# Group A's rotary sums: traced two units later and tied to the instruction ahead of them on their engine

## The chip, the core and the metric

The kernel runs on one core of a Trainium2 chip. A core has a matrix engine (TensorE, PE in the profile, with its weight loads as PEld), three elementwise engines (VectorE as DVE, ScalarE as ACT, GpSimd as POOL), and a queue engine, SyncE (SP), which in this kernel issues most of the DMA transfers. Each engine works through its own list of instructions in order, and an instruction that needs another engine's result waits at the head of that list on a semaphore. The metric is the device time of one execution in microseconds. The program is one two-layer encoder over 512 tokens of width 1024, batch 1.

## What is computed

The reference, cut to the part that the change touches (group A of the even layer):

```
z = h @ w_in
qa, ka, va, cq, ckv, kr = jnp.split(z, EVEN_SPLITS, axis=-1)
qa = axial_rope(rmsnorm(qa.reshape(b, s, A_HEADS, HEAD_DIM), a_q_norm), row, col)
ka = axial_rope(rmsnorm(ka.reshape(b, s, A_KV_HEADS, HEAD_DIM), a_k_norm), row, col)
oa = block_attention(qa, ka, va, HEAD_DIM ** -0.5)     # 8 query heads, 2 key heads, softmax over 512 keys
ob = block_attention(q_full, k_full, vb, ...)          # group B, 8 heads from low-rank latents cq, ckv, kr
h = h + concat(oa, ob) @ w_out
h = h + sq_relu_mlp(rmsnorm(h, norm_ffn[layer]), ...)
...
rope: x * cos + swap(x) * sin, swap exchanging the halves of each rotary pair
```

The odd layer (neighbourhood attention) and both MLPs follow, then a final norm. The change alters no arithmetic.

## The kernel before

All products are done in three passes of a rounded part and its remainder (`hi`, `lo`), which is why so many instructions come in pairs: a copy on ScalarE that rounds, and a subtraction on VectorE that keeps what was lost.

**Units.** `attend` runs heads in units of 128 queries: unit n = 4 x head + block, so group A's eight heads are units 0 to 31. For each unit the code is written in this order: the score matmuls (line 893, two for group A), the head's `done(i)` callback, the row minimum with scaling on VectorE (897), the exponential on ScalarE (899), the reciprocal (900, VectorE) and the normalisation on GpSimd (901); then the transposes of the unit three back (860 on TensorE, 862 on ScalarE, 863 on VectorE); then, one unit after both halves of a head are there, its value product (873) with the copy (882, ScalarE), the sum (883, VectorE) and, after every second head, the split (742 ScalarE, 743 VectorE); then `step`, which lets a queue of fill work run on for 1.5 us of estimated matmul time. During group A the fill holds the rest of the input projection (matmuls at 426 to 428, evacuations 432, 433, 618 to 621), the rotary key's small product (`rotary_key`, lines 708 to 714, whose weights come by the DMA at 708), the latents (724) and group B's first projections, each with its weight chunks (DMA 180, ScalarE 192 or 202, VectorE or GpSimd 193 or 203).

**The rotary queries.** Eight heads of queries lie in four tiles t = 0 to 3, two heads in each. Tile t+1 is made while the heads of tile t run. `rope_q(t+1)` is traced at the start of head 2t (units 0, 8 and 16 for t+1 = 1, 2 and 3). With `far=True` it fetches the swapped halves with eight DMAs on SyncE (482), multiplies by the cosines into a tile `c` on GpSimd (486) and by the sines into `sh` on GpSimd (487). `sum_q(t+1)` then adds both (547, VectorE), rounds the sum into the query slot (549, ScalarE), takes the remainder (550, VectorE) and rearranges the halves of the partitions with three DMAs on SyncE (551, 552, 553). The third of these writes what the first reads, so it waits for the first to land. The next pair of heads, from unit 8(t+1) on, multiplies by that slot. Before the change `sum_q(t+1)` is traced in the third unit of the even head: units 2, 10 and 18.

**What sets the order.** Nobody writes the order of an engine's list by hand. The tile framework plans it while the program is built: it steps through an estimate of the program's course, and at each point an engine is given, of the instructions that the estimate takes to be ready, the one that was traced first. So an instruction can be placed ahead of others that were traced before it, if the estimate has it ready sooner; on the chip it then holds its list up for as long as its inputs take. `keep_in_program_order` takes part in this planning only: it adds an order edge from the given instruction to the one traced last before it on the same engine, and no wait for a semaphore.

**Shared tiles.** `sh`, `c`, `lo` of the sum, the weights of the rotary key and the pieces of a head's output (882, 883) all come from one pool of six scratch tiles (`sc`). A value product has a single output bank in PSUM (`o`), and scores have two (`s`).

Of the kernel before, what the change touches and what calls it, by code (L numbers as in the profile page):

```python
# [11 lines left out]
AF = mybir.ActivationFunctionType  # L12
ALU = mybir.AluOpType
# [17 lines left out]
def f32(ap):  # L31
    return ap.bitcast(F32)
# [3 lines left out]
def encoder_kernel(ctx: ExitStack, tc: tile.TileContext, ins, out, dbg=None):  # L36
    nc = tc.nc
    PE, ACT, DVE, POOL, SP = nc.tensor, nc.scalar, nc.vector, nc.gpsimd, nc.sync
# [52 lines left out]
    def scratch(dt=F32):  # L91
        return scp.tile([P, 512], dt, tag="sc", name=nm("sc"))
# [436 lines left out]
    def rope_q(t):  # L529


        QA.append(Slot())
        src = QS[t // 2].t[:, S * (t % 2) : S * (t % 2) + S]
        if t:
            hold["rope"] = rope(src, cosA, sinA, sw16, far=True)
            return
        rt = rope(src, cosA, sinA, sw16)
        q = QA[t].pair()
        for e in range(2):
            a, z = 64 * e, 64 * (1 - e)  # L540
            ACT.activation(q[a : a + 64, e, :], rt[a : a + 64, :], AF.Copy)
            DVE.tensor_tensor(q[z : z + 64, e, :], rt[a : a + 64, :], f32(q[a : a + 64, e, :]), op=ALU.subtract)

    def sum_q(t):
        q = QA[t].pair()
        rt, sh = hold["rope"]
        DVE.tensor_tensor(rt, rt, sh, op=ALU.add)
        lo = scratch(F32R)
        ACT.activation(q[:, 0, :], rt, AF.Copy)
        DVE.tensor_tensor(lo, rt, f32(q[:, 0, :]), op=ALU.subtract)  # L550
        SP.dma_start(f32(q[0:64, 1, :]), f32(q[64:128, 0, :]))
        SP.dma_start(f32(q[64:128, 1, :]), f32(lo[64:128, :]))
        SP.dma_start(f32(q[64:128, 0, :]), f32(lo[0:64, :]))
        if t == 3:
            for s_ in QS + [rpA]:
                s_.free()
# [363 lines left out]
    def heads_A():  # L920
        for h in range(8):
            t, e, kv = h // 2, h % 2, h // 4
            if e == 0 and t < 3:
                rope_q(t + 1)
            q, k = QA[t].pair(), KA[kv].pair()

            def done(i, t=t, e=e):
                if e == 0 and t < 3 and i == 2:
                    sum_q(t + 1)
                if i == 3 and e:  # L930
                    QA[t].free()
                    if t % 2:
                        KA[t // 2].free()

            yield dict(e=e, done=done, scale=lambda i, h=h: hold["scA"][:, i, h : h + 1],
                       passes=lambda i, q=q, k=k, e=e: [(q[:, e, i * P : (i + 1) * P], k[:, z, :]) for z in range(2)],
                       vlhs=lambda kt, kv=kv: VAv[:, kt, kv, :], after=VA.free if h == 7 else lambda: None)
# [546 lines left out]
```

## Time and profile before

| | us |
|---|---|
| median of the 3 runs | 1221.71 (1220.49 to 1222.97) |
| the profiled execution, its own time | 1220.6 |
| its span, from first to last instruction | 1218.8 |
| what lies around the span | 1.8 |
| TensorE busy in the span | 1189.6 |
| VectorE / ScalarE / GpSimd busy | 814.0 / 628.3 / 411.5 |
| mean granted TensorE clock | 0.997 |

Times in the views count from the start of the span. A line of the timeline gives the start, the length, the engine, the source line, the operation, what it writes and reads with shapes, a count where equal instructions were merged, and in brackets how long the engine had idled before it and what ended that. A line of the waits gives who waited for whom, the sum in us, how often, and the longest. A row of the table by stretches gives the stretch, its length, and for each engine its busy time and number of instructions, then the granted TensorE clock, the share of the DMA engines in use and the rate.

### The profile page before, as it was taken

The page shows a single profiled execution, that of the slowest core. Times are in us where ns is not written, and L with a number is a line of the kernel's source. Part 1 is how long each engine was busy: PE and PEld are TensorE (multiplying, and loading weights), DVE is VectorE, ACT ScalarE, POOL GpSimd, SP SyncE. Part 2 cuts the span into 40 slices and gives each one's busy share as a digit, 9 for nine tenths or more (in the row PEclk, how much of TensorE's full clock was granted, in tenths as well). Part 3 has the DMA queues.
Part 4 walks back from the last instruction along what each step waited for, and adds up shares of the span by engine and source line. Part 5 has one row for each costly group of instructions (what it writes and reads, how often), then busy time and mean ns, then how long its engine had stood idle before and what let it go on. Part 6 is the DMA issues. An engine that isn't in the chain of part 4 may idle for free.

```text
span 1218.8 us, 18461 instructions
## 1 busy us (share of the span) xinstructions
PE 1189.6 (98%) x6644; PEld 1003.4 (82%) x6644; DVE 814.0 (67%) x1433; ACT 628.3 (52%) x1051; POOL 411.5 (34%) x535
## 2 busy tenths in 40 slices
PE   9998999999999999999999999999999999999997
PEld 8676788887899889898877777778788988988985
DVE  4587888878678338448566677675984763764764
ACT  5576676664446326235445565554563641451553
POOL 3256242205365146155001222111243913623700
PEclk9999999999999999999999999999999999999999
DMA  7223314212224224247224334323221341241332
GB/s 246 65 72 85 75 48 131 69 53 70 78 88 147 87 62 132 101 125 242 91 80 126 108 100 115 111 87 122 69 78 53 97 155 60 87 156 44 122 122 69
DMA packets 107259, 122.69 MB, mean 101 GB/s; under 512 B 8115, under 2 KB 81120, under 8 KB 107168
## 3 DMA queue, kind: packets, MB, share of 16 engines
q1 hardware_dynamic: 104880, 116.15, 30.9%
q0 software_dynamic: 1536, 4.21, 1.5%
q10 hardware_dynamic: 752, 1.15, 0.4%
q8 instruction: 52, 0.85, 0.3%
q14 instruction: 39, 0.32, 0.1%
HBM read 104.32 MB, written 6.29 MB: 91 GB/s over the span
## 4 chain that ended last, share of the span: by engine, by line
PE 78%; DVE 9%; ACT 4%; issue 3%; SPq 2%; POOL 2%; DMA 2%; DVEq 0%; POOLq 0%; ACTq 0%
PE mm L428 7%; PE mm L426 7%; PE mm L427 7%; PE s L428 2%; PE s L427 2%; PE s L426 2%; PE s L893 2%; PE o L873 2%; PE mm L316 2%; PE mm L314 2%; PE mm L315 2%; PE mm L1384 2%; PE mm L1383 2%; PE mm L1382 2%; PE t L860 2%
## 5 line engine op out<-in xcount | busy, mean ns | idle before, releaser
L193 DVE TENSOR_TENSOR wlo<-raw,whi 128x1024 fp32r<-128x1024 f32 (+2 forms) x141 | 158.7, 1127 | 152.7 <-ACT whi L192 149.5
L192 ACT ACTIVATE whi<-raw 128x1024 fp32r<-128x1024 f32 (+2 forms) x144 | 136.4, 949 | 168.0 <-PE o L427 38.7
L426 PE MATMUL mm<-a,whi 128*128 128x512 f32 x524 | 211.9, 406 | 0.4 <-DVE sc L790 0.4
L427 PE MATMUL mm<-a,whi 128*128 128x512 f32 x524 | 207.7, 396 | 0.1
L428 PE MATMUL mm<-a,wlo 128*128 128x512 f32 x524 | 207.2, 397 | 0.1
L240 DVE TENSOR_TENSOR wlo<-raw,whi 128x896 fp32r<-128x896 f32 x104 | 128.1, 1232 | 106.9 <-ACT whi L239 100.7
L239 ACT ACTIVATE whi<-raw 128x896 fp32r<-128x896 f32 x104 | 98.9, 951 | 161.5 <-PE s L1384 27.7
L234 POOL TENSOR_TENSOR raw<-raw 128x128 f32<-128x128 f32 x104 | 62.4, 600 | 271.5 <-DMA raw<-in_ffn_w_up_dram 204.7
L428 PEld LDWEIGHTS mm<-a,wlo 128*128 128x128 f32 x524 | 98.4, 188 | 23.2 <-issue 1.7
L427 PEld LDWEIGHTS mm<-a,whi 128*128 128x128 f32 x524 | 98.8, 189 | 20.2 <-issue 1.7
L426 PEld LDWEIGHTS mm<-a,whi 128*128 128x128 f32 x524 | 98.6, 188 | 20.3 <-issue 0.9
L236 POOL TENSOR_TENSOR raw<-raw 128x128 f32<-128x128 f32 x104 | 90.7, 872 | 8.1
L235 POOL TENSOR_TENSOR raw<-raw 128x256 f32<-128x256 f32 x104 | 87.9, 845 | 8.2
L1225 POOL TENSOR_SCALAR p<-p,ti 128x256 f32<-128x256 f32 x64 | 35.2, 556 | 134.4 <-DVE ti L1224 112.6
L316 PE MATMUL mm<-a,wlo 128*128 128x256 f32 x280 | 79.0, 282 | 1.6 <-DVE wlo L240 1.6
L315 PE MATMUL mm<-a,whi 128*128 128x256 f32 x280 | 78.6, 281 | 0.0
L314 PE MATMUL mm<-a,whi 128*128 128x256 f32 x280 | 78.6, 281 | 0.0
L901 POOL TENSOR_SCALAR p<-p,ti 128x512 f32<-128x512 f32 x64 | 46.6, 731 | 90.1 <-DVE ti L900 76.3
L316 PEld LDWEIGHTS mm<-a,wlo 128*128 128x128 f32 x280 | 52.8, 188 | 2.6 <-DVE wlo L240 2.6
L314 PE MATMUL t<-a,whi 128*128 128x256 f32 x192 | 53.9, 281 | 0.0
L315 PE MATMUL t<-a,whi 128*128 128x256 f32 x192 | 53.9, 281 | 0.0
L316 PE MATMUL t<-a,wlo 128*128 128x256 f32 x192 | 53.8, 280 | 0.0
(308 smaller groups left out, 3042.9 us busy)
## 6 DMA issues: line engine op xcount, KB each, us to landing
raw<-in_ffn_w_down_dram SPq DMA_DIRECT2D x64, 512.0 KB
raw<-in_ffn_w_up_dram SPq DMA_DIRECT2D x104, 256.0 KB
raw<-in_od_w_qkv_dram SPq DMA_DIRECT2D x64, 192.0 KB
raw<-in_ffn_w_up_dram SPq DMA_DIRECT2D x12, 512.0 KB
raw<-in_ev_w_in_dram SPq DMA_DIRECT2D x12, 384.0 KB
bias<-bx SPq DMA_DIRECT2D x16, 256.0 KB
a<-a POOLq DMA_DIRECT2D x16, 256.0 KB, 3.0
a<-a SPq DMA_DIRECT2D x10, 256.0 KB
```

The source lines that it names most:

```text
L192: ACT.activation(hi[:, 0:m], raw[:, 0:m], AF.Copy)
L193: (eng or DVE).tensor_tensor(lo_[:, 0:m], raw[:, 0:m], f32(hi[:, 0:m]), op=ALU.subtract)
L235: POOL.tensor_tensor(r[:, 4:6], r[:, 2:3].to_broadcast([P, 2, P]), r[:, 0:7:6], op=ALU.add)
L236: POOL.tensor_tensor(r[:, 7], r[:, 3], r[:, 5], op=ALU.subtract)
L239: ACT.activation(hi[:, 0:896], raw[:, 128:1024], AF.Copy)
L240: DVE.tensor_tensor(lo[:, 0:896], raw[:, 128:1024], f32(hi[:, 0:896]), op=ALU.subtract)
L314: PE.matmul(o, wh, x[:, 0], start=kp == 0 and z == 0, stop=False, skip_group_check=True)
L315: PE.matmul(o, wh, x[:, 1], start=False, stop=False, skip_group_check=True)
L316: PE.matmul(o, wl, x[:, 0], start=False, stop=kp == self.np - 1, skip_group_check=True)
L426: PE.matmul(o, wh, xh, start=first, stop=False)
L427: PE.matmul(o, wh, xl, start=False, stop=False)
L428: PE.matmul(o, wl, xh, start=False, stop=last)
```

## The change

`sum_q(t+1)` is called from the first unit of the odd head of tile t (units 4, 12 and 20) in place of the third unit of its even head (units 2, 10 and 18). Its three computing instructions, 547, 549 and 550, are passed through `keep_in_program_order`, so that each is planned behind the instruction traced last before it on VectorE or ScalarE. The three DMAs are not passed through it. `rope_q`, the fill work and the units stay where they are in the code.

```diff
     def sum_q(t):
         q = QA[t].pair()
         rt, sh = hold["rope"]
-        DVE.tensor_tensor(rt, rt, sh, op=ALU.add)
+
+        held = tc.keep_in_program_order
+        held(DVE.tensor_tensor(rt, rt, sh, op=ALU.add))
         lo = scratch(F32R)
-        ACT.activation(q[:, 0, :], rt, AF.Copy)
-        DVE.tensor_tensor(lo, rt, f32(q[:, 0, :]), op=ALU.subtract)
+        held(ACT.activation(q[:, 0, :], rt, AF.Copy))
+        held(DVE.tensor_tensor(lo, rt, f32(q[:, 0, :]), op=ALU.subtract))
         SP.dma_start(f32(q[0:64, 1, :]), f32(q[64:128, 0, :]))
         SP.dma_start(f32(q[64:128, 1, :]), f32(lo[64:128, :]))
         SP.dma_start(f32(q[64:128, 0, :]), f32(lo[0:64, :]))
...
             def done(i, t=t, e=e):
-                if e == 0 and t < 3 and i == 2:
+                if e == 1 and t < 3 and i == 0:
                     sum_q(t + 1)
```

## The prediction

> **What bounds the kernel now.** I read the page first: how busy TensorE is, and whose work the chain of waits is made of.
>
> ```profile
> span 1218.8 us, 18461 instructions
> ...
> PE 1189.6 (98%) x6644; PEld 1003.4 (82%) x6644; DVE 814.0 (67%) x1433; ACT 628.3 (52%) x1051; POOL 411.5 (34%) x535
> ...
> PE 78%; DVE 9%; ACT 4%; issue 3%; SPq 2%; POOL 2%; DMA 2%; DVEq 0%; POOLq 0%; ACTq 0%
> ```
>
> TensorE is busy for 1189.6 of 1218.8 us, so at most 29 us are to be had anywhere, and an edit elsewhere counts by the TensorE time it opens or closes. Group A's units run from about 66 to 157 us. So I cut this part into stretches:
>
> ```profile
> 76.00:82.00 6.00, 6.00 (x38) 4.86 (x37) 5.46 (x16) 5.48 (x14) 3.77 (x6) 1.00 0.32 75
> 82.00:88.00 6.00, 6.00 (x42) 5.37 (x41) 5.42 (x14) 5.56 (x11) 5.05 (x5) 1.00 0.01 1
> 94.00:100.00 6.00, 4.56 (x28) 3.71 (x27) 5.03 (x12) 4.30 (x10) 2.89 (x4) 1.00 0.41 112
> 112.00:118.00 6.00, 3.42 (x17) 2.81 (x15) 4.07 (x9) 3.23 (x8) 3.96 (x5) 0.74 0.33 66
> 117.00:118.00 1.00, 1.00 (x6) 0.54 (x4) 0.79 (x2) 0.74 (x3) 0.74 (x2) 0.50 1.00 198
> 118.00:119.00 1.00, 0.83 (x4) 0.57 (x3) 1.00 (x3) 0.78 (x2) 0.00 (x0) 0.87 0.78 229
> ```
>
> In the first two stretches TensorE has no hole. It is short of 1.44 us in 94 to 100 and of 2.58 us in 112 to 118, and there its clock falls too, to half by 117 to 118. The waits from 64 to 145 us say who is behind it:
>
> ```profile
> DVE sc L547 <- POOL sc L487: 3.8, 2, 2.1
> PE o L873 <- DVE a L863: 2.6, 1, 2.6
> PE o L873 <- DVE sc L883: 1.4, 1, 1.4
> PE s L893 <- DMA a<-sc: 0.2, 1, 0.2
> ```
>
> Both long TensorE waits are for VectorE, and VectorE itself stood twice, for 3.8 us in all, at line 547, the first instruction of the moved step. The timeline of VectorE shows what was queued behind it (the other engines' rows follow where they are used):
>
> ```profile
> 71.67 0.69 DVE L547 TENSOR_TENSOR sc<-sc,sc 128x512 f32<-128x512 f32 x1
> ...
> 76.53 0.69 DVE L863 TENSOR_TENSOR a<-t,a 128x512 fp32r<-128x512 f32 x1
> ...
> 94.91 0.69 DVE L547 TENSOR_TENSOR sc<-sc,sc 128x512 f32<-128x512 f32 x1 [1.74 <-POOL sc L487]
> ...
> 113.33 0.69 DVE L547 TENSOR_TENSOR sc<-sc,sc 128x512 f32<-128x512 f32 x1 [2.08 <-POOL sc L487]
> ...
> 114.01 0.67 DVE L863 TENSOR_TENSOR a<-t,a 128x512 fp32r<-128x512 f32 x1
> ...
> 119.17 0.68 DVE L743 TENSOR_TENSOR a<-sc,a 128x512 fp32r<-128x512 f32 x1
> ```
>
> **Part by part.** No instruction is added or removed: per tile there remain two VectorE instructions, one on ScalarE and three DMAs. The edges cost nothing at run time, being order only. What counts is where the three sums land.
>
> *Tile 3, units 18 to 20.* The sum stood in front of unit 15's remainder (863 at 114.01), which was traced in the same unit 18 but after it. Now it is traced in unit 20 and tied behind the last VectorE instruction of unit 19. That is the split of heads 2 and 3 (743), since unit 19 ends with head 3's value product and its fill is TensorE work alone. So 863 is freed from the 2.08 us.
>
> ```profile
> 111.11 0.59 ACT L862 ACTIVATE a<-t 128x512 fp32r<-128x512 f32 x1
> ...
> 114.05 0.63 ACT L549 ACTIVATE a<-sc 128x512 fp32r<-128x512 f32 x1 [1.65 <-DVE sc L547]
> ```
>
> ```profile
> 105.69 1.19 PE L873 MATMUL o<-a,a 128*128 128x256 f32 x8
> ...
> 114.73 1.78 PE L873 MATMUL o<-a,a 128*128 128x256 f32 x7 [2.58 <-DVE a L863]
> ...
> 118.70 0.74 PE L893 MATMUL s<-a,a 128*128 128x512 f32 x2 [0.17 <-DVE ti L897]
> ...
> 130.23 0.63 PE L893 MATMUL s<-a,a 128*128 128x512 f32 x2
> ```
>
> The next input of 863 is its partner 862, which ends at 111.11 + 0.59 = 111.70. Add 0.67 for 863 and the value product can begin at 112.4 in place of 114.73: 2.3 us earlier. After the gap seven such matmuls took 1.78 us, where eight took 1.19 at full clock. The clock is 0.50 or near it for about 3.3 us, from 115 until into the stretch 118 to 119, so half of that, 1.6 us, is work not done; the part ahead of unit 22's scores (118.70) that lies on the chain is the value product's 0.7 to 0.8 and the transposes behind it, 0.4. I take 2.3 + 1.2 = **3.5 us** off the start of unit 22. Bounds: 2.3 if the clock falls all the same, 2.58 + 1.6 = 4.2 if all of both is won.
>
> [...]
>
> What is late next is tile 3's query, first used by unit 24 (130.23). SyncE's rows:
>
> ```profile
> 73.06 0.50 SPq L551 DMA_DIRECT2D a<-a  x1
> ...
> 75.28 0.46 SPq L553 DMA_DIRECT2D a<-sc  x1
> 75.79 5.01 SPq L482 DMA_DIRECT2D sc<-a  x8
> ...
> 96.29 0.50 SPq L551 DMA_DIRECT2D a<-a  x1
> ...
> 100.16 0.46 SPq L553 DMA_DIRECT2D a<-sc  x1
> ...
> 114.71 0.50 SPq L551 DMA_DIRECT2D a<-a  x1
> 115.26 0.58 SPq L708 DMA_DIRECT2D sc<-in_ev_w_in_dram  x1
> ```
>
> The split at 119.17 moves up by the same 3.5 to 115.7, ends at 116.4, and the sum follows: 0.69 for 547, 0.63 for 549, and 551 issues at 117.7. From 551 to 553 pass 2.22 us (73.06 to 75.28) or 3.87 (96.29 to 100.16), and to the use 2.3 (below). That is 122.2 to 123.9, against unit 24 at 130.23 - 3.5 = 126.7. So 3 us of slack hide the delay: 0. Without that cover it would cost what it is late.
>
> On SyncE the moved DMAs are now traced behind 708, the rotary key's weights (unit 18), which so far queued behind 551. It can go out sooner, and the chunk loads with it. I count that as 0, with a gain of at most 1 us (rotary key's product started 2.5 us behind unit 22). On GpSimd nothing is moved: 486 and 487 stay traced where they were.
>
> *Tile 2, units 10 to 12.* Here the place hardly changes. The sum already stands behind unit 13's minimum (94.91 less the 1.74 of waiting is 93.17, where that ended) because the plan had 487 ready no sooner, and unit 10's remainder, which comes next, is traced in unit 13, still later than 12. So I leave 547 at 94.91 with its wait.
>
> ```profile
> 93.58 1.29 POOL L487 TENSOR_TENSOR sc<-sc,a 128x512 f32<-128x512 f32 x1
> ```
>
> ```profile
> 89.67 0.99 PE L873 MATMUL o<-a,a 128*128 128x256 f32 x7
> ...
> 98.97 2.14 PE L873 MATMUL o<-a,a 128*128 128x256 f32 x16 [1.44 <-DVE sc L883]
> ...
> 102.49 0.70 PE L893 MATMUL s<-a,a 128*128 128x512 f32 x2 [0.22 <-DMA a<-sc]
> ```
>
> ```profile
> 96.77 0.59 ACT L882 ACTIVATE sc<-o 64x512 f32<-64x512 f32 x1
> ```
>
> But there is a second effect. Head 1's product ended at 90.66 and its copy (882) ran only at 96.77, so the one `o` bank was held and head 2's product waited, 1.44 us of it idle. The copy takes a scratch tile, and so does `lo` of the sum, traced in unit 10 ahead of the copy (unit 11); 882 ran beside 550. I read that as tiles handed out in traced order. With the sum traced in unit 12 the copy comes first, and the 1.44 us may go. They do not reach the end: unit 16's scores already waited 0.22 us for 553, issued at 100.16, which is 2.3 us from issue to use. If the query lands no sooner, TensorE only arrives earlier and waits there. I take 0.2 us won. Bounds: 1.44 won, and for each us by which 547 slips, one lost.
>
> *Tile 1, units 2 to 4.* This sum is moved for certain: 547 from 71.67 to behind unit 0's remainder, 76.53 + 0.69 = 77.2. Add 0.69, 0.63, 2.22 and 2.33, and the query is there at 83.0.
>
> ```profile
> 79.22 0.93 PE L893 MATMUL s<-a,a 128*128 128x512 f32 x3
> ...
> 83.77 0.40 PE L426 MATMUL mm<-a,whi 128*128 128x512 f32 x1
> ```
>
> Unit 8 used it at 79.22, so its scores come 3.8 us late, or 2.6 if units 0 to 7 gain the 1.2 us of VectorE time that 547 and 550 give up ahead of them. The cover is transposes, values and projection matmuls which TensorE did from 83.77 on and which need only weights. VectorE and ScalarE are above 5.4 of 6 us busy in these stretches, so they take other work in the same time. I take 0; bounds 3.8 lost (nothing covers it) and 1.2 won.
>
> **Sum.** -3.5 - 0.2 + 0 = -3.7 us, against the profiled execution's 1220.6 (span 1218.8 and 1.8 around it), gives 1216.9. That execution is 1.1 below the runs' median, so in their terms it is 1221.7 - 3.7 = **1218.0 us**.
>
> **Rivals.**
> *More is won.* Tile 2's 1.44 us as well, and 708 early: -3.7 - 1.2 - 1.0 = -5.9, so 1215.8. For it speaks the six-us delay of 882; against it, that unit 16 stays tied to 553.
>
> *Given back.* The 3.5 us at unit 22 are lost again, to a short wait at unit 8 (up to 3.8) or because the plan puts another waiting instruction in 547's place. The plan is made anew from unit 2 on, and 547 waited only because its estimate differed from the chip. Net within 2 us: 1221.
>
> *Slower: tile 2's query comes late.* The eight far copies for tile 2 (482 at 75.79) follow 553 of tile 1 in SyncE's list. If they go out 5 us later with it, the plan sets 487 some 5 us further back in GpSimd's list, and 547, 553 and unit 16 with it. TensorE then stands at 102.5 for 5 us, longer than the 2.58 that were followed by half clock, so 1.6 us more: +6.6 - 3.7 = +2.9, 1224.6. Against it: the copies would still land by 88, well ahead of 93.58, so only the plan's estimate can do it. For it: 553 and 482 stand back to back. It decides from a delay of about 4.5 us on, where 4.5 + 1.6 exceeds 3.7 by the 2.4 us below.
>
> *The change does nothing* where plan and traced order already agree, as for tile 2. For tile 3 that fails only if 743 is not what 547 is tied behind; it is counted with "given back".
>
> **Chances.** A measurement of this kernel tells 0.2%, 2.4 us, from no change. The forecast (1216.5 to 1219.2) has 0.42, more won 0.13, given back 0.15, slower 0.30, because a new plan over some 90 us of closely coupled lists can set a wait anywhere. Faster is 0.42 + 0.13 = 0.55. The range 1214.5 to 1225.0 leaves out the far ends of the first and last rival, about 0.15 together.
>
> **What would show it.** Right: no VectorE wait for 487 in front of unit 15's remainder, clock 1.00 in 112 to 118, unit 22's scores near 115, 547 of tile 3 behind the 743, unit 24 without a wait for a DMA; head 1's 882 near 91. Wrong: a wait of scores on `a<-sc` over 1 us at unit 8 or 16, a new stall of over 2 us on VectorE with TensorE behind it, or a stretch beyond 157 us longer by as much as the first part is shorter.

## The result, and the profile after

| | before | changed |
|---|---|---|
| median of 11 runs each, us | 1221.88 (1220.49 to 1227.6) | 1217.92 (1216.35 to 1220.86) |
| ratio to before | | 0.9963 (0.995 to 0.9977) |
| the profiled execution, us | 1220.6 | 1217.92 |

The forecast was 1218.0 us. In the changed kernel every line from 547 on stands two lower in the code, so 547 of before is 549 there, 863 is 865, 873 is 875, 882 is 884 and 893 is 895; GpSimd's 487 keeps its number.

The page of the changed kernel, its span, busy times and chain of waits:

```profile
span 1216.1 us, 18473 instructions
...
PE 1187.8 (98%) x6644; PEld 1001.9 (82%) x6644; DVE 819.5 (67%) x1433; ACT 628.7 (52%) x1051; POOL 417.9 (34%) x535
...
PE 75%; DVE 13%; ACT 5%; issue 3%; POOL 1%; DMA 1%; SPq 1%; DVEq 0%; ACTq 0%; POOLq 0%
```

TensorE has the same 6644 matmuls and was busy 1.8 us less; the span is 2.7 us shorter. VectorE is busy 5.5 us more with the same number of instructions, of which the sum at 93.53 (below) is 1.1. The stretches of the prediction, now of the changed kernel:

```profile
76.00:82.00 6.00, 4.99 (x33) 4.12 (x32) 5.89 (x17) 6.00 (x14) 2.77 (x4) 1.00 0.27 61
82.00:88.00 6.00, 5.74 (x37) 4.53 (x35) 5.29 (x15) 5.95 (x15) 5.13 (x5) 1.00 0.22 51
94.00:100.00 6.00, 4.92 (x29) 3.94 (x28) 5.79 (x12) 3.38 (x9) 2.03 (x3) 1.00 0.51 145
112.00:118.00 6.00, 5.11 (x25) 3.42 (x26) 5.24 (x13) 5.18 (x12) 5.79 (x7) 1.00 0.12 42
```

In 112 to 118 TensorE works 5.11 us instead of 3.42, at clock 1.00 instead of 0.74. In 76 to 88, where it had no hole, it now lacks 1.27 us. The hole in 94 to 100 is 1.08 us, from 1.44. The waits from 64 to 145 us say whom TensorE stood for, and whether VectorE still stands at the sum (549):

```profile
PE o L875 <- DVE a L865: 2.0, 3, 1.1
DVE sc L549 <- POOL sc L487: 0.5, 1, 0.5
PE mm L716 <- DVE a L712: 0.4, 1, 0.4
```

Of VectorE's 3.8 us in front of the sum 0.5 is left, and TensorE's single wait of 2.6 us for the remainder (863 before) has become three of 2.0 in all. The three sums on VectorE's timeline, with what stands next to the second and third:

```profile
76.64 0.82 DVE L549 TENSOR_TENSOR sc<-sc,sc 128x512 f32<-128x512 f32 x1
...
93.53 1.76 DVE L549 TENSOR_TENSOR sc<-sc,sc 128x512 f32<-128x512 f32 x1 [0.51 <-POOL sc L487]
95.21 0.68 DVE L745 TENSOR_TENSOR a<-sc,a 128x512 fp32r<-128x512 f32 x1
95.81 0.15 DVE L902 RECIPROCAL ti<-ti 128x1 f32<-128x1 f32 x1
95.89 0.66 DVE L865 TENSOR_TENSOR a<-t,a 128x512 fp32r<-128x512 f32 x1
...
111.89 0.74 DVE L433 SCALAR_TENSOR_TENSOR a<-mm,gT,a 128x512 fp32r<-128x512 f32 x1
112.62 0.67 DVE L865 TENSOR_TENSOR a<-t,a 128x512 fp32r<-128x512 f32 x1
...
118.04 0.89 DVE L745 TENSOR_TENSOR a<-sc,a 128x512 fp32r<-128x512 f32 x1 [0.51 <-ACT a L744]
118.86 0.68 DVE L549 TENSOR_TENSOR sc<-sc,sc 128x512 f32<-128x512 f32 x1
```

Tile 3's sum stands behind the split of heads 2 and 3 (745), and unit 15's remainder (865) runs at 112.62 without a wait. Behind tile 2's sum stand the split of heads 0 and 1 and then the remainder of an earlier unit. TensorE's timeline shows what followed:

```profile
80.34 0.63 PE L862 MATMUL t<-cst,p 128*128 128x128 f32 x4 [0.52 <-DVE ti L902]
...
81.57 1.11 PE L875 MATMUL o<-a,a 128*128 128x256 f32 x7 [0.49 <-DVE a L865]
...
83.31 1.17 PE L895 MATMUL s<-a,a 128*128 128x512 f32 x4
...
96.61 1.10 PE L875 MATMUL o<-a,a 128*128 128x256 f32 x7 [1.08 <-DVE a L865]
...
113.35 0.62 PE L875 MATMUL o<-a,a 128*128 128x256 f32 x3 [0.46 <-DVE a L865]
114.37 1.15 PE L716 MATMUL mm<-a,a 128*64 128x512 f32 x4 [0.41 <-DVE a L712]
...
123.69 0.62 PE L895 MATMUL s<-a,a 128*128 128x512 f32 x2
...
127.41 0.63 PE L895 MATMUL s<-a,a 128*128 128x512 f32 x2
```

The value product begins at 113.35 (114.73 before), but what follows it is not unit 22's scores (118.70 before, 123.69 now): the rotary key's product (716, 714 before) has come forward from 121.18 to 114.37. SyncE's timeline shows that its weights came earlier:

```profile
109.06 0.58 SPq L710 DMA_DIRECT2D sc<-in_ev_w_in_dram  x1
...
120.23 0.50 SPq L553 DMA_DIRECT2D a<-a  x1
...
122.45 0.46 SPq L555 DMA_DIRECT2D a<-sc  x1
```

They go out at 109.06, where they had gone at 115.26 behind the sum's first DMA; what had kept them back is seen below, in the kernel whose `lo` has a tile of its own. Unit 24, the first use of tile 3's query, starts at 127.41 (130.23 before) and waits for no transfer.

**Where on the way the time was won.** The table below is worked out from the traces. For each kernel the columns streamed by its matmuls (512 for an output of 128x512) are added up in order, and the time at which the running total reaches what before had reached at a given time is compared with that time; the offset at 30 us, ahead of the change, is taken off. Negative is ahead of before. The kernels do the same work in different orders, so the table is read only at times at which all of them have done the same work: there, counting matmuls instead of columns gives the same figures.

```
us of before      70     92    110    180 |  600   1200 | 110 to 180
changed        +0.01  +1.28  +0.46  -2.57 | -2.68  -2.93 |  -3.03
changed_again  +0.00  +1.28  +0.47  -2.53 | -2.83  -2.55 |  -3.00
tile3_only     -0.01  +0.03  -0.36  -3.37 | -1.59  -0.23 |  -3.01
tiles23_only   -0.01  +0.05  -0.86  -3.93 | -3.14  -2.96 |  -3.07
move_only      -0.01  +0.31  -1.49  -4.03 | -4.03  -3.17 |  -2.54
move23         +0.01  +0.04  -0.53  -3.11 | -2.57  -2.51 |  -2.58
own_lo         -0.01  +0.02  -0.97  -1.74 | -1.53  -0.05 |  -0.77
sines_vector   -0.02  -0.02  +0.23  -0.52 | -0.47  -0.53 |  -0.75
pin_only       +0.03  +0.77  +0.11  -0.50 | +0.17  +0.46 |  -0.61
wait_back      -0.02  +0.89  -1.30  -1.68 | -0.66  +0.41 |  -0.38
tiles12_only   +0.00  +1.29  +0.48  +0.76 | -0.14  +0.85 |  +0.28
warm_gap       +0.00  +0.04  +0.15  +0.14 | +0.79  +1.11 |  -0.01
```

The first row: 1.3 us lost by 92 (tile 1), 0.8 won back to 110 (the stretch of tile 2), 3.0 won to 180 (tile 3). The other rows are the kernels of the next section, in this order: the changed kernel run again; tile 3 alone; tiles 2 and 3 alone; the later call without the tie, for all tiles and for tiles 2 and 3; `lo` in a tile of its own; tile 3's sines on VectorE; the ties alone; the wait put back; tiles 1 and 2 alone; matmuls laid into the gap (not counted here). Two pairs of rows part tiles 1 and 2 in another way, at 110: `changed` and `tiles23_only` differ in tile 1 alone and stand 1.3 apart, `tiles23_only` and `tile3_only` differ in tile 2 alone and stand 0.5 apart. The expectations below speak of 0.8 us lost at tile 1; that was read at 90 us, where the kernels have not done the same work. Beyond 180 us nothing was changed and single profiles still drift by up to 3 us, so times rest on medians of five rounds, and rows only on what they show up to 180.

### The profile page after: what moved, and what is told of

Read it like the earlier page. It is cut to its first block, busy times and chain, and to the rows that moved or that the text cites. A ratio compares the mean times of both kernels' runs of the same rounds, so it can differ in the third digit from the quotient of the medians.

```text
span 1216.1 us, 18473 instructions
## 1 busy us (share of the span) xinstructions
PE 1187.8 (98%) x6644; PEld 1001.9 (82%) x6644; DVE 819.5 (67%) x1433; ACT 628.7 (52%) x1051; POOL 417.9 (34%) x535
## 4 chain that ended last, share of the span: by engine, by line
PE 75%; DVE 13%; ACT 5%; issue 3%; POOL 1%; DMA 1%; SPq 1%; DVEq 0%; ACTq 0%; POOLq 0%
PE mm L426 7%; PE mm L428 7%; PE mm L427 7%; PE s L428 2%; PE s L426 2%; PE s L427 2%; PE mm L316 2%; PE mm L314 2%; PE mm L315 2%; PE s L895 2%; DVE wlo L193 2%; PE t L314 2%; PE t L315 2%; PE t L316 2%; PE mm L1386 2%
## 5 line engine op out<-in xcount | busy, mean ns | idle before, releaser
L234 POOL TENSOR_TENSOR raw<-raw 128x128 f32<-128x128 f32 x104 | 68.3, 656 | 264.4 <-DMA raw<-in_ffn_w_up_dram 172.2
L235 POOL TENSOR_TENSOR raw<-raw 128x256 f32<-128x256 f32 x104 | 97.3, 935 | 8.1
L236 POOL TENSOR_TENSOR raw<-raw 128x128 f32<-128x128 f32 x104 | 81.1, 779 | 8.1
```

Of the source, the lines that this page charges most:

```text
L235: POOL.tensor_tensor(r[:, 4:6], r[:, 2:3].to_broadcast([P, 2, P]), r[:, 0:7:6], op=ALU.add)
L236: POOL.tensor_tensor(r[:, 7], r[:, 3], r[:, 5], op=ALU.subtract)
```

## The experiments

Each kernel was timed in five rounds against the kernel before on the same chip. The theory: VectorE's wait for 487 at tile 3's sum cost about 3.6 us, tile 1's later sum costs about 1 us, and the later call, not the tie, does the work. The main rivals: the ties do it, or the gain comes from elsewhere on the way.

### Tile 3 alone, and tiles 1 and 2 alone

```diff
-        held = tc.keep_in_program_order
+        held = tc.keep_in_program_order if t in (3,) else lambda ins: ins
...
-                if e == 1 and t < 3 and i == 0:
+                if t < 3 and (e, i) == ((1, 0) if t + 1 in (3,) else (0, 2)):
```

The second kernel has `(1, 2)` in place of `(3,)`.

> Only tile 3's sum is moved and tied; tiles 1 and 2 are summed where they were. Theory (the gain is the 2.58 us TensorE gap in front of head 3's value product and the half clock behind it, both from tile 3's sum): 1218.5, ratio 0.9972; no VectorE wait for 487 in front of unit 15's remainder, granted clock 1.00 from 112 to 118, the 1.44 us wait in 94 to 100 still there. Rival (the gain is tile 2's: the copy 882 that waited for a scratch tile): 1221.9, ratio 1.000.

> Tiles 1 and 2 are moved and tied, tile 3's sum stays. Theory (tile 3): 1221.9 within 0.7, ratio 1.000; the 2.1 us VectorE wait for 487, a TensorE gap of about 2.6 us behind it and a clock below 1 are still there, while head 1's copy runs near 91 and the 1.44 us wait in 94 to 100 is smaller. Rival (tile 2): 1218.5, ratio 0.997.

Measured: tile 3 alone 1218.45 us, ratio 0.9978 (0.9969 to 0.9987); tiles 1 and 2 alone 1222.63, ratio 1.0014 (1.0005 to 1.0022), both against 1221.15. The stretch of tile 3's sum with tile 3 alone:

```profile
112.00:118.00 6.00, 5.35 (x28) 3.62 (x29) 5.21 (x13) 4.70 (x11) 5.07 (x6) 1.00 0.12 33
```

and with tiles 1 and 2 alone, the stretch and the sum itself on VectorE's timeline:

```profile
112.00:118.00 6.00, 3.37 (x16) 2.88 (x16) 3.41 (x10) 3.45 (x8) 4.21 (x5) 0.81 0.19 38
```

```profile
114.14 0.69 DVE L549 TENSOR_TENSOR sc<-sc,sc 128x512 f32<-128x512 f32 x1 [2.08 <-POOL sc L487]
```

With tiles 1 and 2 alone the 2.08 us of waiting and the clock below 1 are there as before; with tile 3 alone both are gone. So the gain sits in tile 3, and tiles 1 and 2 together cost 0.5 us at 110 and 1.5 in the median.

### The later call without the tie, and the tie without the later call

```diff
-        held = tc.keep_in_program_order
+        held = lambda ins: ins
```

and, in the other kernel,

```diff
-                if e == 1 and t < 3 and i == 0:
+                if e == 0 and t < 3 and i == 2:
```

> All three sums two units later, none tied. Theory (the place of tile 3's sum in VectorE's list matters, and the later call alone puts it behind unit 15's remainder): 1218.9, ratio 0.9975, with at most 0.6 us of VectorE waiting for 487, now in front of unit 16's remainder. Rival (the order edges do it): 1221.9, ratio 1.000, with the 2 us wait back.

> All three sums tied, called where they were. Theory (place): 1221.9 within 0.7, ratio 1.000, both waits of 1.7 and 2.1 us for 487 and the gap of 2.6 us still there, since the edges reach back only to work that stood ahead anyway. Rival (the edges do it): 1218.5, ratio 0.997.

Measured: the call alone 1217.36, ratio 0.9969 (0.9956 to 0.9981); the ties alone 1221.81, ratio 1.0004 (0.9996 to 1.0012). VectorE in the kernel with the call alone, tile 1's and tile 3's sum, and then its stretch of 94 to 100:

```profile
71.67 0.69 DVE L549 TENSOR_TENSOR sc<-sc,sc 128x512 f32<-128x512 f32 x1
...
112.11 1.10 DVE L549 TENSOR_TENSOR sc<-sc,sc 128x512 f32<-128x512 f32 x1
```

```profile
94.00:100.00 6.00, 6.00 (x35) 5.10 (x34) 5.64 (x15) 4.74 (x12) 3.65 (x5) 1.00 0.49 134
```

Untied, the plan puts tile 1's sum exactly where before had it, at 71.67, and 0.31 us are lost at 92, not 1.28; tile 3's sum runs at 112.11 with no wait, since it now comes behind unit 15's remainder by its place in the code. The hole in 94 to 100 is closed. With the ties alone, at the old call (VectorE, then TensorE):

```profile
112.89 0.69 DVE L549 TENSOR_TENSOR sc<-sc,sc 128x512 f32<-128x512 f32 x1 [2.03 <-POOL sc L487]
```

```profile
114.29 1.09 PE L875 MATMUL o<-a,a 128*128 128x256 f32 x7 [2.52 <-DVE a L865]
...
117.72 0.74 PE L895 MATMUL s<-a,a 128*128 128x512 f32 x2 [0.34 <-DVE ti L899]
```

The wait and the gap are back. The later call carries the gain; in the medians the ties add nothing measurable to it. On the way they cost 1.0 at tile 1 (1.28 against 0.31 at 92), while at tile 3 the tied kernels win 3.0 and the untied ones 2.5. This kernel's gap of 2.52 us was not followed by half clock (1.00 in 112 to 118), which the next sections use.

### Tiles 2 and 3, tied and untied

The kernels are as "tile 3 alone" with `(2, 3)`; the second has `held = lambda ins: ins` as well.

> Tiles 2 and 3 moved and tied, tile 1's sum where it was. Theory (moving tile 1 cost 0.8 us, through unit 8's late scores, and disturbed tile 2's place): unit 8's scores near 79, no TensorE wait for 885 in 94 to 100, and about 5 us off by 125 us of the span: 1216.5, ratio 0.996. Rival (tile 1's move costs nothing, as the prediction had it): as the changed kernel, 1218, ratio 0.997.

> Sums of tiles 2 and 3 two units later, tile 1 as before, nothing tied. Theory (later call does it, ties and tile 1's move are dispensable): 1217.5, ratio 0.9965, and by 125 us of the span some 4 us ahead of before. Rival (ties or tile 1 are needed): ratio 0.998 or above.

Measured: tied 1218.71, ratio 0.9974 (0.9965 to 0.9984); untied 1217.26, ratio 0.9961 (0.9948 to 0.9974). In both traces tile 1's 1.3 us are not lost (+0.05 and +0.04 at 92). The time of the tied one missed the 1216.5 that was expected, although it is 3.93 ahead at 180. The intervals of both overlap the changed kernel's (0.995 to 0.9977): that leaving tile 1 alone is worth anything at the end is not shown.

### The sum's `lo` in a tile of its own

```diff
-        lo = scratch(F32R)
+        lo = scp.tile([P, 512], F32R, tag="bias", bufs=2, name=nm("lo"))
```

on the kernel before.

> The kernel before with one edit: the remainder of the sum comes from a tile of its own pool tag (two tiles that this layer leaves unused) in place of the six scratch tiles. Theory (head 1's copy 882 was late because the scratch tile of the sum, traced ahead of it, had to be handed out first): 882 runs near 91 in place of 96.77 and the 1.44 us wait in 94 to 100 goes or shrinks; the 2.6 us gap near 112 stays; 1221.0, ratio 0.999 to 1.000. Rival (882 is late for another reason): 882 at 96.8, the wait unchanged, ratio 1.000.

Measured: 1221.36 against 1221.69, ratio 1.0 (0.9992 to 1.0009). Head 1's copy on ScalarE's timeline, the rotary key's weights on SyncE's, and TensorE's gap at tile 3:

```profile
90.59 0.59 ACT L882 ACTIVATE sc<-o 64x512 f32<-64x512 f32 x1
```

```profile
106.01 0.53 SPq L708 DMA_DIRECT2D sc<-in_ev_w_in_dram  x1
```

```profile
113.14 1.10 PE L873 MATMUL o<-a,a 128*128 128x256 f32 x5 [2.58 <-DVE a L863]
```

The copy runs at 90.59 instead of 96.77, and 0.97 us are won by 110. So `lo`, handed out ahead of it from the same pool, is what had held the copy up, as the prediction read it. The rotary key's weights, which take a scratch tile too, go out at 106.01 instead of 115.26, although the sum and its DMAs are called where they were. So it was the scratch tile of `lo` that had kept them back, and not their place behind the sum in SyncE's queue. The 2.58 us at tile 3 stay, and nothing is left at the end.

### Tile 3's sines on VectorE

```diff
-        (POOL if far else DVE).tensor_tensor(sh[0:n, :], sh[0:n, :], sin[0:n, :], op=ALU.mult)
+        (by or (POOL if far else DVE)).tensor_tensor(sh[0:n, :], sh[0:n, :], sin[0:n, :], op=ALU.mult)
...
-            hold["rope"] = rope(src, cosA, sinA, sw16, far=True)
+            hold["rope"] = rope(src, cosA, sinA, sw16, far=True, by=DVE if t == 3 else None)
```

on the kernel before, with `by=None` as a new argument of `rope`. The sum stays where it is and has nothing of GpSimd's to wait for.

> The kernel before with tile 3's product by the sines (487) on VectorE in place of GpSimd; the sum keeps its place in front of unit 15's remainder. Theory (what cost was the wait for GpSimd at that place): VectorE no longer waits there, value product of head 3 near 113, 2 to 3 us off: 1219, ratio 0.998. Rival (the place itself, two more instructions ahead of the remainder, costs as much): 1221.9, ratio 1.000.

Measured: 1220.95 against 1221.69, ratio 0.9998 (0.999 to 1.0007). VectorE, then TensorE:

```profile
110.97 1.11 DVE L487 TENSOR_TENSOR sc<-sc,a 128x512 f32<-128x512 f32 x1
...
112.66 1.10 DVE L547 TENSOR_TENSOR sc<-sc,sc 128x512 f32<-128x512 f32 x1
```

```profile
114.48 1.09 PE L873 MATMUL o<-a,a 128*128 128x256 f32 x7 [1.63 <-DVE a L863]
```

The run does not separate the two. The wait was swapped for 2.21 us of VectorE's own work at the same place, ahead of the remainder, and the value product moved only from 114.73 to 114.48. It does say that taking GpSimd out of the chain is worth little while the work stands in front of the remainder.

### Matmuls laid into the gap

```diff
         o = h["o"]
+            if half and len(O) == 1 and h["e"]:
+                for _ in range(6):
+                    tc.keep_in_program_order(PE.matmul(o[:, 256:384], ones, ones, start=True, stop=True, skip_group_check=True))
```

on the kernel before; the result of the added products is overwritten by the value product.

> The kernel before with six 128x128 products of ones, whose result is overwritten, on TensorE ahead of head 3's second value product, some 2.7 us of work in the 2.58 us gap. Theory of the forecast (half clock behind the gap costs 1.2 us on the path): the product still starts at 114.7, clock 1.00 from 112 to 118, unit 22's scores 1.2 us earlier, 1220.7, ratio 0.999. Rival (VectorE and ScalarE set the pace there, as a 2.5 us gap without a fall of the clock showed): unit 22 at most 0.6 us earlier, ratio 1.000.

Measured: 1222.08 against 1221.69, ratio 1.0006 (0.9997 to 1.0014). TensorE's timeline, and a stretch behind the gap:

```profile
110.90 1.50 PE L873 MATMUL o<-ones 128*128 128x128 f32 x12
...
115.01 1.76 PE L876 MATMUL o<-a,a 128*128 128x256 f32 x7 [2.02 <-DVE a L863]
```

```profile
116.00:117.00 1.00, 1.00 (x7) 1.00 (x7) 0.88 (x3) 0.19 (x1) 0.95 (x1) 0.50 0.69 148
```

The six calls left twelve records and took 1.50 us, not the 2.7 that was expected, and they were done before the gap had well begun; 2.02 us of it remained, and the clock fell all the same. On the price of the clock the run by itself says little; that half clock followed a gap of 2.02 us is used below.

### The wait put back into the changed kernel

```diff
             def done(i, t=t, e=e):
+                if e == 0 and t == 2 and i == 2:
+                    DVE.tensor_copy(tiny(1), hold["rope"][1][:, 0:1])
                 if e == 1 and t < 3 and i == 0:
                     sum_q(t + 1)
```

A copy of one column of `sh` at the old place of tile 3's sum (line 931): it has to wait for 487 as the sum did, and does 0.15 us of work.

> The changed kernel with one more VectorE instruction: a copy of one column of sh for tile 3, called in unit 18 where the sum was called before, so that VectorE waits for 487 in front of unit 15's remainder and does nearly nothing there. Theory (the wait at that place is what tile 3's move won): a wait of 1.5 to 2 us for 487 is back, head 3's value product starts 1.5 to 2 us later than in the changed kernel, and 1.5 to 2.5 us of the gain go: 1220.3, ratio 0.998 to 0.9995. Rival (the work of 549 and 552 at that place, not the wait): as the changed kernel, ratio 0.9965.

> The changed kernel once more beside the two others: ratio 0.9963 within its interval (0.995 to 0.9977); in the trace again about 0.8 us lost by unit 8 and 3 to 4 us won between 106 and 125.

Measured on one chip: wait put back 1220.33, ratio 0.9986 (0.9977 to 0.9995); the changed kernel again, 1217.99, ratio 0.9962 (0.9949 to 0.9974), both against 1222.56. With the wait put back, VectorE and TensorE:

```profile
112.20 0.15 DVE L931 COPY ti<-sc 128x1 f32<-128x1 f32 x1 [2.08 <-POOL sc L487]
```

```profile
113.73 0.62 PE L875 MATMUL o<-a,a 128*128 128x256 f32 x3 [2.70 <-DVE a L865]
```

The 2.08 us are there to the digit, TensorE stands for 2.70 us, and of the 3.0 us that every kernel with a tied later sum wins from 110 to 180 this one wins 0.4. Sum, ties and DMAs are called as in the changed kernel, and the rotary key's product comes early as there (114.19). So this wait, at this place, is what tile 3's gain consists of, some 2.6 us of it. The medians differ by 2.34 us, and their intervals do not meet. The traces alone would not give that: at 180 the two are 0.9 apart, since the plan with the copy had won 1.8 us more ahead of 110, and the rest of the difference lies beyond 180, where this profile lost 1.3 us to half clock near 869 (mean clock 0.78 in 868 to 871, 0.65 in 871 to 874).

## Why the prediction was right, step by step

**Tile 3, -3.5: right in size** (-3.0 from 110 to 180; -3.4 in all where tile 3 alone is moved), and tested from three sides: not there with tile 3 left out, gone again with the wait put back, and won by the later call without the tie. The way to it was in part another. The remainder could run at 112.62, not 111.7, since an evacuation (433) was planned in front of it and the changed kernel was by then 0.7 us later (unit 21's scores at 112.03, 111.30 before). The gap in front of the value product shrank from 2.58 to 0.46 us, 2.1 of the 2.3 foreseen; on the clock of the trace the product came only 1.4 earlier. The other 0.9 lies behind it, in the clock and in a new order, which no run separates. The prediction had seen that the rotary key's weights would go out sooner, put it down to SyncE's queue, where `own_lo` shows the scratch tile, and counted it as nothing, at most 1 us. That is near what the early product can be worth: `own_lo` and `wait_back` have it as well and win 0.8 and 0.4. That the product would overtake unit 22's scores, the prediction did not see, so its mark "unit 22 near 115" failed.

**The clock's 1.2 in it** is the least certain number. Two kernels that had the gap but no half clock behind it won 0.6 (ties alone, gap 2.52 us, clock 1.00) and 0.4 (wait put back, 2.70 us, 1.00) on before from 110 to 180, which would put the half clock's part near 0.5. But of three more with the gap and the half clock, one won 0.8 (its own `lo`), one nothing (matmuls in the gap) and one lost 0.3 (tiles 1 and 2 alone), so other shifts of the plan are as large and the split is open.

**Tile 3's delay hidden by 3 us of slack: right.** Its sum ran at 118.86 (116.4 foreseen), its last DMA at 122.45, and unit 24 did not wait.

**Tile 2, -0.2: near in size, by a swap of terms.** From 92 to 110 the changed kernel wins 0.8, but tile 3 alone wins 0.4 there too; with and without tile 2 the kernels stand 0.5 apart. The early copy came as read (884 in the changed kernel):

```profile
90.92 0.59 ACT L884 ACTIVATE sc<-o 64x512 f32<-64x512 f32 x1
```

But the 1.44 us it freed were not lost at unit 16, as the prediction had it; unit 16 had no wait for a DMA. Most of them were lost in VectorE's list: the sum took 1.76 us instead of 0.69, the split (745, 0.68) came next, and only then the remainder (865) for which TensorE waited 1.08 us at 96.61.

**Tile 1, 0: the mis-sized term.** It lost 1.3, within the bounds of 1.2 won and 3.8 lost. Unit 8's scores came at 83.31, where the arithmetic had the query at 83.0; the fill covered most of the 4 us, not all: the row of 76 to 82 lacks 1.01 us of TensorE. VectorE and ScalarE were busy 5.89 and 6.00 of 6 us there, which points to them as what held the fill back. The kernel with the call alone shows that it is the tie that sends this sum back (71.67 without it, 76.64 with it); "moved for certain" was true of the tied call only.

**The rivals.** "More is won" came about for tile 2 only in the kernel with the call alone (-1.8 from 92 to 110) and in the one with the wait put back (-2.2). "Given back" happened with 1.3 at tile 1. Tile 2's query was not late. "The change does nothing" fell with the ratio.

**The sum.** -3.7 was foreseen; the steps measure +1.28 - 0.82 - 3.03 = -2.57 in the profiled executions, and the medians differ by 1221.88 - 1217.92 = 3.96. The 1.4 us between them are not in any step. So the mechanism and the size of tile 3 were right, but that 1218.0 met 1217.92 so closely is luck: the 1.3 us that tile 1 lost and these 1.4 us cancel. One thing bears on the 1.4 us: a stretch of half clock of 3.413 us takes 0.0014 off the mean clock (3.413 / 2 / 1218.8). Nine of the changed kernel's 11 runs have a mean clock of 0.998 or more, as its profile, which has no such stretch before its end; of the 80 runs of before in the experiments 4 have, and 54 have 0.995 or 0.996, below the 0.997 of before's profile with its one stretch. By that estimate most runs of before would have more than one such stretch. Where these lie in runs without a profile is open.

## What to carry to other kernels

When an engine's list is planned from estimates, look for the wait at the head of the list whose own result is needed late, and count what stands behind it: here 2.08 us on VectorE, for a sum first used 17 us later, were 2.58 us of TensorE. Moving its call in the code behind the urgent work was enough; a hard tie did not shorten the median, and cost 1.0 us on the way where the plan had been right. And count a moved step's buffers with it: when its scratch tile was handed out later, a copy and another product's weights came 6 us sooner.

## What the hardware showed that was not expected

**The granted clock changed at whole multiples of 3.4133 us.** In the clock record of before's trace it is full for 109.226 us from its first rise on, half for 3.413 and full again for 1095.677: 32, 1 and 321 times 3.4133. In the changed kernel's it is full for 1204.905, 353 times. In all 13 traces each change of the clock, counted from its first rise to full, comes at such a multiple; the first rise itself comes anywhere from 4.10 to 6.54 us after the start of the span. Where it fell behind the gap at tile 3 it fell at the 32nd, 109.226 us after the rise, in all four kernels, and for 3.413 us each time. In these seven kernels what goes with it is how much of the gap lay between two neighbouring multiples, not its length; worked out from the traces, beside the mean clock of the stretch from 112 to 118 us:

```
kernel          gap, us   most of it between two multiples   clock   half clock behind it
before            2.58              2.58                      0.74           yes
own_lo            2.58              2.58                      0.72           yes
tiles12_only      2.6               2.57                      0.81           yes
warm_gap          2.02              2.02                      0.76           yes
wait_back         2.70              1.82                      1.00           no
pin_only          2.52              1.62                      1.00           no
sines_vector      1.63              1.42                      1.00           no
```

A gap of 2.70 us across a multiple was not followed by half clock, one of 2.02 between two of them was. Why is not shown. Nor does the idle time between two multiples by itself part the cases: near 867 us, in other work, 0.92 to 1.03 us without a matmul were followed by half clock in five kernels (mean clock from 868 to 871: 0.50 with `lo` in a tile of its own, 0.70 with tile 3 alone, 0.78 with the wait put back), and 0.91 to 0.95 not in five others (0.95 in before, 0.93 in the changed kernel, clock 1.00 in both). There each fall cost 1.26 to 1.29 us on the scale of the table above, from 860 to 880 us.

**The sums that ran beside an instruction of GpSimd took longer, but for one.** The 13 traces have 39 of these sums on VectorE, all alike (547 or 549). In 24 GpSimd ran nothing meanwhile, and each of them took 0.68 or 0.69 us. In 15 it ran an instruction: one of these took 0.67, the other 14 from 0.82, with 0.28 us of GpSimd's work beside it, to 1.77, with 1.22. Tile 2's sum in the changed kernel took 1.76 us from 93.53 on; GpSimd's timeline has this meanwhile:

```profile
92.21 1.29 POOL L487 TENSOR_TENSOR sc<-sc,a 128x512 f32<-128x512 f32 x1
93.46 1.28 POOL L193 TENSOR_TENSOR wlo<-raw,whi 128x512 fp32r<-128x512 f32 x1
```

GpSimd's 193 runs from 93.46 to 94.74 and the sum ends at 95.29, 0.55 us behind it, not much less than the 0.68 or 0.69 that a sum took with GpSimd idle. Why the sum takes longer then is not shown. A sum that is moved should be looked at for what it then runs beside: here 1.76 us in place of 0.69.
